# The low part of every weight split: 11/16 of the columns on VectorE, 5/16 on GpSimd

## The chip, the cores and the metric

The kernel runs on one core of one Trainium2 chip. The metric is the device time of a run in microseconds (us), taken as the median of three runs.

## What is computed

Two transformer blocks of two layers each, one after the other, on 256 tokens of 2048 features, everything in float32. Cut to what matters here:

```python
# first block, per layer
mod = silu(c) @ w_mod + b_mod                    # shift, scale, gate: c is one vector
h = rms_norm(x, g_pre) * (1 + scale) + shift
proj = h @ w_in                                  # 2048 x 5648
y = concat(sliding_window_attention, spatial_gating, gated_linear_attention) * silu(z)
x = x + gate * rms_norm(y @ w_out, g_post)
# second block, per layer
proj = rms_norm(x) @ w_in_2
x = x + concat(mla, differential, banded attention) @ w_o_2
h = rms_norm(x)
x = x + square(relu(h @ w_up_2)) @ w_down_2      # 2048 x 8192 and back
```

The weights are read once; with 256 tokens each weight is used for two token tiles of 128.

## The kernel before

**The products.** A float32 product is made of three faster ones. Each operand is split into a high part (hi, the value rounded to the type `fp32r`) and a low part (lo, the value less hi), and `three` (L285) adds hi x hi, hi x lo and lo x hi into one bank of PSUM (lines L287, L288, L289; L288 is the one that reads the weight's lo). In the MLP's `up` the weight is the stationary operand, and lines L1190 (hi) and L1192 (lo) do the same in two matmuls. Five of the 16 K tiles of the first layer are not split and go whole through L325.

**The weight units.** `w_unit` (L269) fetches two K tiles (128 rows each) times n columns (512, 288 or 264) into one raw tile [128, 1024] and calls `split` (L262), which makes hi on ScalarE (L265) and lo on VectorE (L266):

```python
        A.copy(out=hi[:, :n], in_=src)
        V.tensor_tensor(out=lo[:, :n], in0=src, in1=hi[:, :n].bitcast(F32), op=SUB)
```

There are 964 such splits. raw has 5 buffers, hi and lo have 3 each, so ScalarE and VectorE can be at most three units ahead of TensorE, and a raw buffer is free for the next load once its hi and lo are made. SP issues all of these loads from one queue, in order.

**The background work.** Beside the products of the first block, `gemv` (L475) computes the modulation vectors of the next stage on VectorE: it loads w_mod into rawm (2 buffers, the same SP queue, L485) and multiplies and adds into gacc (L491, L493), with both inputs in SBUF. `pump` gives out such a load after every four K tiles.

**Who else uses GpSimd.** `rstd` (L237) takes its power there (L241, 128x1 or 128x4), and four affine selects (L846) mask the spatial gate's weights; a few small loads are issued from its queue.

**What sets the order.** The program is written layer by layer, but the order in which each engine gets its instructions is made by a scheduler from its own estimates, so that a changed instruction can move its neighbours. All engines then run in their own order and wait for each other through semaphores.

Of the kernel before, what the change touches and what calls it, by code (L numbers as in the profile page):

```python
# [11 lines left out]
F32 = mybir.dt.float32  # L12
# [6 lines left out]
PSUM = bass.MemoryType.PSUM  # L19
# [71 lines left out]
def kernel(  # L91
# [36 lines left out]
    def gate_load(t, on):  # L128
        """a load into t waits for what on waits for."""
        V.tensor_copy(out=t[0:1, 0:1], in_=on)  # L130
# [4 lines left out]

    # ---------------------------------------------------------------- constants
    C_RES = C_SWA
# [17 lines left out]

    # vectors that scale features, feature-major
    fm = const.tile([P, 3 * P], F32, name="fm")
    fmap = {}

    def fm_load(g, parts, on=None):  # L160
        """parts: (names, [rows, 128] AP); the rows become columns of fm, from 128 g on."""
        st = tm("y")
        if on is not None:
            gate_load(st, on)
        n = 0
        for names, ap in parts:
            r = ap.shape[0]
            (nc.sync if g == 0 else nc.scalar).dma_start(out=st[n:n + r, :P], in_=ap)
            for i, name in enumerate(names):
                fmap[name] = g * P + n + i * (r // len(names))  # L170
            n += r
        pb = bank()
        PE.transpose(pb[:, :n], st[:n, :P], ident[:n, :n])
        V.tensor_copy(out=fm[:, g * P:g * P + n], in_=pb[:, :n])
# [17 lines left out]

    # vectors along the free axis
    sink_bc = const.tile([P, DEPTH, 16], F32, name="sink_bc")
# [34 lines left out]

    # ---------------------------------------------------------------- helpers  # L230
    def copy(eng, out, in_):
# [12 lines left out]
    def put(dst, ps, scale=None):  # L244
        """dst (hi | lo) from a [128, 256] view of PSUM."""
        hi, lo = dst[:, 0, :], dst[:, 1, :]
        if scale is None:
            A.copy(out=hi, in_=ps)
            V.tensor_tensor(out=lo, in0=ps, in1=hi.bitcast(F32), op=SUB)
        else:  # L250
            A.activation(out=hi, in_=ps, func=AF.Copy, scale=scale)
            V.scalar_tensor_tensor(out=lo, in0=ps, scalar=scale, in1=hi.bitcast(F32), op0=MUL, op1=SUB)  # L252
# [6 lines left out]
    def raw_tile(tag="raw"):  # L259
        return wp.tile([P, 1024], F32, tag=tag, bufs={"raw": 5, "rawm": 2}[tag], name=f"{tag}{next(uid)}")  # L260

    def split(src, n):  # L262
        hi = wp.tile([P, 1024], F32R, tag="hi", name=f"hi{next(uid)}")
        lo = wp.tile([P, 1024], F32R, tag="lo", name=f"lo{next(uid)}")
        A.copy(out=hi[:, :n], in_=src)  # L265
        V.tensor_tensor(out=lo[:, :n], in0=src, in1=hi[:, :n].bitcast(F32), op=SUB)  # L266
        return hi, lo

    def w_unit(w, k0, n0, n, whole=()):  # L269
        """4 K tiles x n columns of w, split but for those in whole; yields (kt, [(hi [128, n], lo), ...])."""  # L270
        for k in range(k0, k0 + 4, 2):
            raw = raw_tile()
            nc.sync.dma_start(
                out=raw[:, :2 * n].rearrange("p (k n) -> p k n", k=2),
                in_=w[k * P:(k + 2) * P, n0:n0 + n].rearrange("(k p) n -> p k n", p=P))
            js = [j for j in range(2) if k + j not in whole]
            parts = [(raw[:, j * n:(j + 1) * n], None) for j in range(2)]
            if js:
                o = js[0] * n
                hi, lo = split(raw[:, o:o + len(js) * n], len(js) * n)  # L280
                for i, j in enumerate(js):
                    parts[j] = hi[:, i * n:(i + 1) * n], lo[:, i * n:(i + 1) * n]
            yield (k, parts)

    def three(ps, xa, xb, wh, wl, first, last):  # L285
        """(xa + xb)^T (wh + wl) onto ps."""
        PE.matmul(ps, lhsT=xa, rhs=wh, start=first, stop=False)  # L287
        PE.matmul(ps, lhsT=xa, rhs=wl, start=False, stop=False)  # L288
        PE.matmul(ps, lhsT=xb, rhs=wh, start=False, stop=last)  # L289
# [4 lines left out]
    def settle(age=0):  # L294
        """the last step of each gemv whose loads were all given out at least age pumps ago."""
        while late and bg["n"] - late[0][0] >= age:
            late.pop(0)[1]()
# [42 lines left out]
    def softmax(ps, nh, nk, bias, scale, sink=None, rd=None):  # L340
        """ps [128, nh, nk]; bias: list of (head slice, AP); e = exp(s - max), 1 / sum.

        A sink is one more score, which no value goes with."""
        w = nk if sink is None else nk + 1
# [16 lines left out]
    def turn(srcs, eng, m=None, tag="k"):  # L361
        """transposes of up to 4 [128, 128] APs, side by side."""
        pb = bank()
        for j, a in enumerate(srcs):
            if m is None:
                PE.transpose(pb[:, j * P:(j + 1) * P], a, ident)  # L366
            else:
                PE.matmul(pb[:, j * P:(j + 1) * P], lhsT=a, rhs=m, start=True, stop=True)
        o = tm(tag)
        copy(eng, o[:, :len(srcs) * P], pb[:, :len(srcs) * P])  # L370
        return o

    def y_turn(dst, ytm):
        """ytm: per token tile a [128, 512]; dst: 4 act tiles."""
        for jj in range(0, 4, 2):
# [9 lines left out]
    def x_done(t, n):  # L385
        """the sum of squares of a finished 512-column piece of x."""
        if n == 0:
            ssx[t] = small(4)
        j = junk
        A.activation(out=j, in_=X[t][n], func=AF.Square, accum_out=ssx[t][:, n:n + 1])  # L390
# [5 lines left out]

    # rotary tables of the first block
    rope = const.tile([P, 2, 2, 16], F32, name="rope")
# [60 lines left out]
    def rotate(buf, nh, cos2, sin2, hf):  # L459
        """in place on buf [128, nh, 2 * hf]; sin2 = (-sin | sin)."""  # L460
        m1 = half_tile() if nh * 2 * hf <= S else tm("s")
# [9 lines left out]

    # ---------------------------------------------------------------- modulation
    mod = {}

    def gemv(l, part, k0, nk, eng, tag, into=None):  # L475
        """columns of (shift, scale, gate)[part] for K tiles k0 .. k0 + nk, feature-major; yields per load."""
        if (l, part) not in mod:
            mod[l, part] = const.tile([P, KT], F32, name=f"mod{l}_{part}")
        n = nk * P
        per = 1024 // n  # L480
# [32 lines left out]
    def gemv_pe(l, part, k0, nk, tag, pb):  # L513
        """the same on the tensor engine, a K tile of the result after the other, into a bank."""
        for i in range(nk):
# [10 lines left out]

    # ---------------------------------------------------------------- first block
    def swa_keys(kv):
# [8 lines left out]
    def swa(l, cc, q, kv, kT, zs, yT):  # L537
        """heads 8 cc .. 8 cc + 7."""
        ys = []
# [34 lines left out]
    def gla(l, qk, vg, cg, zs, yT):  # L574
# [35 lines left out]
        def decay(lv):  # L610
            """exp of level lv's exponents, [128 (head pair's keys), (tile, pair), token]."""
            eb = bank()
# [81 lines left out]
    def head_norm(hs, gain, z=None):  # L694
        """rms over each of 4 [128, 128] APs, times gain (times z)."""
        j = junk
# [44 lines left out]
    def make_hT(l, n, rb, hT, whole):  # L741
        """K tiles 4 n .. 4 n + 3 of the modulated, normalised x, feature-major."""
        for jj in range(0, 4, 2):
# [18 lines left out]
    def block1(l, phases, split_k, order, prepare, need_gate, whole=()):  # L762
# [19 lines left out]
        def places(name, t, ps):  # L782
            """where the columns of a chunk go: (name, tile, source)."""
            if name == "v0":
# [130 lines left out]

    # ---------------------------------------------------------------- second block
    def x_turn(n, gname, dst):
        """K tiles 4 n .. 4 n + 3 of x times a gain, feature-major."""
        for jj in range(0, 4, 2):
# [10 lines left out]
    def attend(nheads, score, bias, scale, vals, dst, m=None):  # L930
        """softmax attention over chunk-causal keys; outputs feature-major, 128 values per head."""
        for h0 in range(0, nheads, 4):
# [27 lines left out]
    def block2(l, xT, r):  # L960
        # c_q, c_kv, k_rope
        units = (0, 4, 8, 12)
# [118 lines left out]

        # differential heads
        for j in range(1, 3):
# [46 lines left out]

        # banded heads, queries of a tile in reverse order
        pr = [[None] * 3 for _ in range(2)]
# [38 lines left out]

        # MLP
        r2 = []
# [58 lines left out]
    def small2(t):  # L1232
        """(cos | cos | -sin | sin) of the second block's rotary positions."""
        o = rope2_t[t]
        return o
# [13 lines left out]

    # ---------------------------------------------------------------- the stack  # L1250
    spill = dr.tile([S, D], F32, name="spill")
# [119 lines left out]
```

## Time and profile before

| what | us |
|---|---|
| median of 3 runs | 3048.32 |
| lowest and highest run | 3045.58, 3050.96 |
| profiled execution, span from its first to its last instruction | 3045.1 |

For the profiled execution the profile gives the span alone; it lies 3.2 us under the median. All times of the trace are microseconds from the start of that span. The first block takes 0 to about 915 us, the first layer of the second block 915 to about 1980 us (its MLP from about 1225 on) and the last layer the rest (its MLP from about 2285 on). In the rows, PE is TensorE's matmuls and PEld its weight loads, DVE is VectorE, ACT ScalarE, POOL GpSimd, SP the engine whose queue issues the loads. A matmul's shown length includes its way through the array, so consecutive ones overlap; their pace is the distance of their starts.

### The profile page before, as it was taken

The numbers are of one execution on the slowest core, as the hardware profiler recorded it, in microseconds if no ns is written. First come the engines' busy times: TensorE is split into PE (matmuls) and PEld (weight loads), VectorE is DVE, ScalarE is ACT, GpSimd is POOL, SyncE is SP. The second block draws the span as 40 slices with busy tenths as digits, with TensorE's granted clock in tenths as the row PEclk, the third lists the DMA queues.
The fourth block names the chain that finished last, engine by engine and source line by source line (L and its number), as shares of the span: only waits on it lengthen the run. The fifth ranks groups of instructions, "written<-read, shape, count | busy, mean of one in ns | idle before, by whom it ended". The sixth has DMA issues, their size and how long they took to land.

```text
span 3045.1 us, 40015 instructions
## 1 busy us (share of the span) xinstructions
PE 2953.5 (97%) x15042; PEld 2442.3 (80%) x15042; DVE 1984.3 (65%) x2832; ACT 1436.1 (47%) x2271; POOL 36.3 (1%) x56
## 2 busy tenths in 40 slices
PE   6999998999999999999999999999999999999998
PEld 5676676887787887888888888888788888888887
DVE  5888877788766555565666656656555665656655
ACT  2334545445556555454444444455554444444444
POOL 0000000000000000000000000000000000000000
PEclk9999998999999999999999999999999999999999
DMA  8898588898454655565665566554556666555564
GB/s 286 291 317 291 184 266 288 279 309 269 123 180 146 180 145 163 175 188 192 189 191 188 190 190 190 190 173 135 166 165 199 192 188 190 190 190 190 188 191 153
DMA packets 318072, 617.57 MB, mean 203 GB/s; under 512 B 20233, under 2 KB 48069, under 8 KB 317877
## 3 DMA queue, kind: packets, MB, share of 16 engines
q1 hardware_dynamic: 317220, 614.40, 63.4%
q8 instruction: 118, 1.93, 0.3%
q0 software_dynamic: 336, 0.49, 0.1%
q14 instruction: 78, 0.63, 0.1%
q10 hardware_dynamic: 320, 0.12, 0.0%
HBM read 610.73 MB, written 4.19 MB: 202 GB/s over the span
## 4 chain that ended last, share of the span: by engine, by line
PE 80%; DMA 8%; DVE 7%; issue 2%; ACT 2%; POOL 0%; SPq 0%; DVEq 0%; ACTq 0%; POOLq 0%
PE b L288 16%; PE b L289 16%; PE b L287 16%; PE b L1190 16%; PE b L1192 8%; DMA rawm<-in_w_mod_dram 5%; DVE gacc L493 2%; DVE lo L266 2%; PE b L325 1%; DMA raw<-in_w_in_dram 1%; PE b L366 1%; ACT hi L265 1%; PE b L564 1%; PE b L952 1%; PE b L551 0%
## 5 line engine op out<-in xcount | busy, mean ns | idle before, releaser
L266 DVE TENSOR_TENSOR lo<-raw,hi 128x1024 fp32r<-128x1024 f32 (+4 forms) x964 | 1126.6, 1170 | 799.0 <-ACT hi L265 795.7
L265 ACT CAST hi<-raw 128x1024 fp32r<-128x1024 f32 (+4 forms) x964 | 972.7, 1009 | 1313.5 <-PE b L289 758.1
L287 PE MATMUL b<-hi,act 128*128 128x512 f32 (+2 forms) x2728 | 1072.9, 394 | 9.2 <-DVE pr L821 2.6
L288 PE MATMUL b<-lo,act 128*128 128x512 f32 (+2 forms) x2728 | 1047.7, 384 | 6.9 <-DVE lo L266 6.8
L289 PE MATMUL b<-hi,act 128*128 128x512 f32 (+2 forms) x2728 | 1045.5, 384 | 0.3 <-DVE act L252 0.3
L1190 PE MATMUL b<-act,hi 128*128 128x512 f32 x2048 | 721.0, 397 | 0.0
L287 PEld LDWEIGHTS b<-hi,act 128*128 128x128 f32 x2728 | 515.1, 189 | 121.2 <-issue 16.4
L288 PEld LDWEIGHTS b<-lo,act 128*128 128x128 f32 x2728 | 515.7, 189 | 117.1 <-DVE lo L266 11.7
L289 PEld LDWEIGHTS b<-hi,act 128*128 128x128 f32 x2728 | 514.9, 189 | 98.1 <-issue 1.2
L1192 PE MATMUL b<-act,lo 128*128 128x256 f32 x2048 | 574.9, 281 | 0.0
L1190 PEld LDWEIGHTS b<-act,hi 128*128 128x128 f32 x2048 | 384.4, 188 | 92.8
L1192 PEld LDWEIGHTS b<-act,lo 128*128 128x128 f32 x2048 | 386.9, 189 | 0.5
L493 DVE SCALAR_TENSOR_TENSOR gacc<-rawm,sc,gacc 128x1024 f32<-128x1024 f32 (+1 forms) x210 | 220.9, 1052 | 57.7 <-DMA rawm<-in_w_mod_dram 56.2
L325 PE MATMUL b<-raw,act 128*128 128x512 f32 (+1 forms) x240 | 111.0, 561 | 0.0
L1208 DVE SCALAR_TENSOR_TENSOR act<-b,s,act 128x512 f32<-128x512 f32 x128 | 90.0, 744 | 5.7 <-PE b L289 5.7
L354 ACT ACTIVATE s<-s,s 128x128 f32<-128x128 f32 (+3 forms) x144 | 64.1, 447 | 40.3 <-DVE s L351 39.3
L241 POOL TENSOR_TENSOR s<-s,cs 128x1 f32<-128x1 f32 (+1 forms) x38 | 27.6, 730 | 2909.0 <-DVE s L239 2709.3
L325 PEld LDWEIGHTS b<-raw,act 128*128 128x128 f32 x240 | 43.8, 191 | 17.9 <-issue 11.8
L1200 DVE SCALAR_TENSOR_TENSOR h<-h 128x256 f32<-128x256 f32 x128 | 54.4, 425 | 4.4
L821 DVE TENSOR_TENSOR act<-b,act 128x512 f32<-128x512 f32 (+2 forms) x82 | 51.4, 632 | 8.2 <-PE b L325 7.4
L390 ACT ACTIVATE junk<-act 128x512 bf16<-128x512 f32 x56 | 35.1, 626 | 40.2 <-DMA act<-in_x_dram 21.1
L1198 DVE TENSOR_TENSOR h<-b,h 128x256 f32<-128x256 f32 x128 | 53.4, 417 | 0.0
(268 smaller groups left out, 1666.7 us busy)
## 6 DMA issues: line engine op xcount, KB each, us to landing
raw<-in_w_in_dram SPq DMA_DIRECT2D x256, 512.0 KB, 4.8
raw<-in_w_up_dram SPq DMA_DIRECT2D x256, 512.0 KB, 3.7
raw<-in_w_down_dram SPq DMA_DIRECT2D x256, 512.0 KB, 3.6
rawm<-in_w_mod_dram SPq DMA_DIRECT2D x176, 512.0 KB, 4.8
raw<-in_w_out_dram SPq DMA_DIRECT2D x64, 512.0 KB, 4.7
raw<-in_w_o_dram SPq DMA_DIRECT2D x64, 512.0 KB, 3.7
raw<-in_w_in_dram SPq DMA_DIRECT2D x32, 288.0 KB, 2.9
raw<-in_w_in_dram SPq DMA_DIRECT2D x32, 264.0 KB, 4.7
```

Of the source, the lines that this page charges most:

```text
L265: A.copy(out=hi[:, :n], in_=src)
L266: V.tensor_tensor(out=lo[:, :n], in0=src, in1=hi[:, :n].bitcast(F32), op=SUB)
L287: PE.matmul(ps, lhsT=xa, rhs=wh, start=first, stop=False)
L288: PE.matmul(ps, lhsT=xa, rhs=wl, start=False, stop=False)
L289: PE.matmul(ps, lhsT=xb, rhs=wh, start=False, stop=last)
L325: PE.matmul(ps[t][:, :n], lhsT=a[:, t * P:(t + 1) * P], rhs=wh, start=kk + j == units[0], stop=kk + j == units[-1] + 3)
L354: A.activation(out=s[:, h, :], in_=s[:, h, :], func=AF.Exp, bias=nm[:, h:h + 1], accum_out=den[:, h:h + 1])
L493: eng.scalar_tensor_tensor(out=acc, in0=w, scalar=sc[:, u + k:u + k + 1], in1=acc, op0=MUL, op1=ADD)
L1190: PE.matmul(ps[f], lhsT=wh[:, f * P:(f + 1) * P], rhs=a.rearrange("p a b -> p (a b)"), start=(kk + j == 0), stop=False)
L1192: PE.matmul(ps[f][:, S:], lhsT=wl[:, f * P:(f + 1) * P], rhs=a[:, 0, :], start=False, stop=(kk + j == KT - 1))
L1200: V.scalar_tensor_tensor(out=s2, in0=s, scalar=0.0, in1=s, op0=MAX, op1=MUL)
L1208: V.scalar_tensor_tensor(out=xc, in0=ps, scalar=r2[t], in1=xc, op0=MUL, op1=ADD)
```

## The change

`split` is the only place that changes in what is executed. m is 704 of 1024 columns, 352 of 512, 363 of 528 and 182 of 264; VectorE subtracts those and GpSimd the last 320, 160, 165 or 82. Below this place the lines of the changed kernel are 5 higher, the hi copy is L267, VectorE's subtract L269 and GpSimd's L271. The rest of the diff removes comments and docstrings.

```diff
+    POOL_PART = 5
+
     def split(src, n):
         hi = wp.tile([P, 1024], F32R, tag="hi", name=f"hi{next(uid)}")
         lo = wp.tile([P, 1024], F32R, tag="lo", name=f"lo{next(uid)}")
         A.copy(out=hi[:, :n], in_=src)
-        V.tensor_tensor(out=lo[:, :n], in0=src, in1=hi[:, :n].bitcast(F32), op=SUB)
+        m = n - n * POOL_PART // 16
+        V.tensor_tensor(out=lo[:, :m], in0=src[:, :m], in1=hi[:, :m].bitcast(F32), op=SUB)
+        if m < n:
+            G.tensor_tensor(out=lo[:, m:n], in0=src[:, m:], in1=hi[:, m:n].bitcast(F32), op=SUB)
         return hi, lo
```

The order of instructions changes too. GpSimd's queue, late in the first layer, before (powers for a norm, two selects, two powers):

```order
14 L241 TENSOR_TENSOR s_2675<-s_2673,cs 128x4
15 L241 TENSOR_TENSOR s_2690<-s_2688,cs 128x4
16 L846 AFFINE_SELECT s_3234<-s_3234 128x512
17 L846 AFFINE_SELECT s_3245<-s_3245 128x512
18 L241 TENSOR_TENSOR s_3272<-s_3270,cs 128x1
19 L241 TENSOR_TENSOR s_3296<-s_3294,cs 128x1
```

And the same place of the changed kernel:

```order
94 L241 TENSOR_TENSOR s_2763<-s_2761,cs 128x4
95 L271 TENSOR_TENSOR lo_3201<-raw_3198,hi_3200 128x320
96 L271 TENSOR_TENSOR lo_3220<-raw_3217,hi_3219 128x160
97 L271 TENSOR_TENSOR lo_3246<-raw_3243,hi_3245 128x320
98 L271 TENSOR_TENSOR lo_3265<-raw_3262,hi_3264 128x160
99 L271 TENSOR_TENSOR lo_3286<-raw_3283,hi_3285 128x320
100 L851 AFFINE_SELECT s_3318<-s_3318 128x512
101 L851 AFFINE_SELECT s_3329<-s_3329 128x512
102 L271 TENSOR_TENSOR lo_3423<-raw_3420,hi_3422 128x320
103 L241 TENSOR_TENSOR s_3356<-s_3354,cs 128x1
104 L271 TENSOR_TENSOR lo_3442<-raw_3439,hi_3441 128x320
105 L241 TENSOR_TENSOR s_3380<-s_3378,cs 128x1
```

The subtracts of all 964 splits now stand between the powers and the selects, in one queue with them.

TensorE, one unit in the second layer of the first block, before, with the semaphores that a matmul waits for:

```order
1679 L287 MATMUL b_4284<-hi_4288,act_4231 128x512 [waits Activation_49]
1680 L288 MATMUL b_4284<-lo_4289,act_4231 128x512
1681 L289 MATMUL b_4284<-hi_4288,act_4231 128x512 [waits DVE_49]
1682 L287 MATMUL b_4284<-hi_4288,act_4236 128x512 [waits Activation_49]
1683 L288 MATMUL b_4284<-lo_4289,act_4236 128x512
```

And a unit at about the same place in the changed kernel (L292 to L294 are the three matmuls):

```order
1716 L292 MATMUL b_4400<-hi_4465,act_4392 128x512 [waits Activation_49]
1717 L293 MATMUL b_4400<-lo_4466,act_4392 128x512 [waits DVE_49]
1718 L294 MATMUL b_4400<-hi_4465,act_4392 128x512 [waits DVE_49]
1719 L292 MATMUL b_4400<-hi_4465,act_4397 128x512 [waits Activation_49]
1720 L293 MATMUL b_4400<-lo_4466,act_4397 128x512 [waits Pool_49]
```

The wait for GpSimd stands at the second matmul that reads lo, three matmuls after the first.

SP's queue of loads in the first layer, before:

```order
66 L273 DMA raw_884<-in_w_in_dram 128x2x512
67 L273 DMA raw_912<-in_w_in_dram 128x2x512
68 L485 DMA rawm_856<-in_w_mod_dram 128x2x512
69 L485 DMA rawm_898<-in_w_mod_dram 128x2x512
70 L273 DMA raw_930<-in_w_in_dram 128x2x512
71 L273 DMA raw_956<-in_w_in_dram 128x2x512
72 L485 DMA rawm_902<-in_w_mod_dram 128x2x512
```

And now:

```order
66 L278 DMA raw_905<-in_w_in_dram 128x2x512
67 L490 DMA rawm_876<-in_w_mod_dram 128x2x512
68 L278 DMA raw_934<-in_w_in_dram 128x2x512
69 L490 DMA rawm_920<-in_w_mod_dram 128x2x512
70 L278 DMA raw_953<-in_w_in_dram 128x2x512
71 L490 DMA rawm_924<-in_w_mod_dram 128x2x512
72 L278 DMA raw_980<-in_w_in_dram 128x2x512
```

Pairs of raw loads and pairs of rawm loads have become single ones in turn, so every second raw load stands one place later.

## Rows read from the trace of the kernel before

**Rows 1.** The page, part 1: busy us (share of the span) xinstructions.

```profile
PE 2953.5 (97%) x15042; PEld 2442.3 (80%) x15042; DVE 1984.3 (65%) x2832; ACT 1436.1 (47%) x2271; POOL 36.3 (1%) x56
```

**Rows 2.** Windows by stage: length, busy us by engine, granted clock, DMA share, GB/s.

```profile
76.00:915.00 839.00, 802.58 (x4030) 623.22 (x4030) 668.05 (x1047) 398.66 (x692) 16.43 (x21) 0.98 0.77 254
915.00:1225.00 310.00, 296.76 (x1614) 251.28 (x1613) 184.24 (x306) 174.37 (x345) 6.95 (x10) 0.98 0.53 157
1225.00:1980.00 755.00, 755.00 (x3808) 639.60 (x3807) 453.49 (x555) 338.42 (x440) 1.11 (x2) 1.00 0.60 189
```

**Rows 3.** Chain of waits, 76 to 915 us: share of the stretch by line.

```profile
by line: DMA rawm<-in_w_mod_dram 19.5%; PE b L288 8.8%; PE b L289 8.5%; PE b L287 8.5%; DVE gacc L493 7.6%; issue 6.3%; DVE lo L266 5.1%; DMA raw<-in_w_in_dram 4.8%; PE b L325 4.1%; PE b L564 2.0%; ACT hi L265 1.8%; PE b L551 1.7%; PE b L36
```

**Rows 4.** Waits of the SP queue, 76 to 915 us: us, times, longest.

```profile
SPq L273 <- DVE lo L266: 227.1, 121, 5.5
SPq L485 <- DVE gacc L493: 191.3, 107, 8.0
```

**Rows 5.** Waits for lo of TensorE's loads and matmuls, 76 to 915 us.

```profile
PEld b L288 <- DVE lo L266: 11.5, 15, 2.4
...
PE b L288 <- DVE lo L266: 6.8, 8, 1.9
```

**Rows 6.** Groups by form, VectorE, 76 to 915 us: busy us, mean ns, idle before.

```profile
L266 DVE TENSOR_TENSOR lo<-raw,hi 128x1024 fp32r<-128x1024 f32 x168 | 204.3, 1219 | 46.2 <-ACT hi L265 45.4
L493 DVE SCALAR_TENSOR_TENSOR gacc<-rawm,sc,gacc 128x1024 f32<-128x1024 f32 x120 | 153.6, 1280 | 45.8 <-DMA rawm<-in_w_mod_dram 45.4
L493 DVE SCALAR_TENSOR_TENSOR gacc<-rawm,sc,gacc 128x512 f32<-128x512 f32 x75 | 56.0, 747 | 9.7 <-DMA rawm<-in_w_mod_dram 9.0
...
L266 DVE TENSOR_TENSOR lo<-raw,hi 128x512 fp32r<-128x512 f32 x26 | 17.8, 684 | 3.5 <-ACT hi L265 3.3
...
L266 DVE TENSOR_TENSOR lo<-raw,hi 128x528 fp32r<-128x528 f32 x23 | 15.9, 700 | 2.1 <-ACT hi L265 2.1
...
L266 DVE TENSOR_TENSOR lo<-raw,hi 128x264 fp32r<-128x264 f32 x5 | 2.1, 428 | 0.8 <-ACT hi L265 0.8
```

**Rows 7.** Timeline, 390 to 396 us: start, us, engine line op; selects and a gacc.

```profile
392.84 0.64 POOL L846 TENSOR_SCALAR_AFFINE_SELECT s<-s 128x512 f32<-128x512 f32 x1 [28.82 <-DMA s<-in_sg_w_dram]
...
394.03 1.28 DVE L493 SCALAR_TENSOR_TENSOR gacc<-rawm,sc,gacc 128x1024 f32<-128x1024 f32 x1 [1.61 <-DMA rawm<-in_w_mod_dram]
...
394.90 0.91 POOL L846 TENSOR_SCALAR_AFFINE_SELECT s<-s 128x512 f32<-128x512 f32 x1 [1.42 <-DMA s<-in_sg_w_dram]
```

**Rows 8.** Timelines of GpSimd and VectorE: powers under a gacc and without.

```profile
518.33 0.55 POOL L241 TENSOR_TENSOR s<-s,cs 128x1 f32<-128x1 f32 x1 [113.08 <-DVE s L907]
1128.49 1.02 POOL L241 TENSOR_TENSOR s<-s,cs 128x4 f32<-128x4 f32 x1 [121.02 <-DVE s L239]
799.62 1.28 DVE L493 SCALAR_TENSOR_TENSOR gacc<-rawm,sc,gacc 128x1024 f32<-128x1024 f32 x1
799.85 1.92 POOL L241 TENSOR_TENSOR s<-s,cs 128x4 f32<-128x4 f32 x1 [271.93 <-DVE s L239]
```

**Rows 9.** The same about 519.6 us: a power under a two-input L911.

```profile
519.64 0.74 DVE L911 SCALAR_TENSOR_TENSOR act<-act,s,act 128x512 f32<-128x512 f32 x1
519.80 0.99 POOL L241 TENSOR_TENSOR s<-s,cs 128x1 f32<-128x1 f32 x1 [0.93 <-DVE s L239]
```

**Rows 10.** Timeline of TensorE in an MLP: first and last of 13 starts in turn.

```profile
1504.07 0.39 PE L289 MATMUL b<-hi,act 128*128 128x512 f32 x1
...
1506.79 0.39 PE L289 MATMUL b<-hi,act 128*128 128x512 f32 x1
```

**Rows 11.** Timelines of ScalarE and VectorE in the same MLP.

```profile
1501.77 1.05 ACT L265 CAST hi<-raw 128x1024 fp32r<-128x1024 f32 x1 [1.67 <-PE b L289]
1500.14 1.23 DVE L266 TENSOR_TENSOR lo<-raw,hi 128x1024 fp32r<-128x1024 f32 x1 [1.49 <-ACT hi L265]
```

**Rows 12.** Waits, 915 to 1225 us: us, times, longest.

```profile
DVE lo L266 <- ACT hi L265: 76.6, 64, 6.0
```

## The prediction

> **What bounds the kernel now.** I read the page's busy shares first. TensorE is busy 97% of the span, VectorE 65%, ScalarE 47%, GpSimd 1% [rows 1]. Work taken off VectorE can therefore pay only where VectorE, and not TensorE, sets the pace, and the windows by stage say where that is [rows 2]. In the first MLP (1225 to 1980 us) TensorE has not one idle microsecond: 755.00 busy of 755.00. In the attention part ahead of it (915 to 1225) it idles 13.2 us. The last layer repeats both from 1980 us on. In the first block's two layers, 76 to 915 us, it idles 36.4 of 839 us, VectorE is busy 668 us (80%) and the DMA engines 77%. I call this stretch stage A; it is the only one with something to win or lose.
>
> The chain of waits inside stage A [rows 3] agrees: a loop of gate-vector loads (rawm, 19.5%) and the multiply-adds that free them (gacc, 7.6%) carries more of it than any matmul line; the low parts (lo) carry 5.1%. The SP queue's own waits show the loop from the other side [rows 4]: it stood 227.1 us until a lo had freed a raw buffer and 191.3 us until a gacc had freed a rawm buffer. TensorE itself hardly waits for a lo: 6.8 us in 8 waits, and 11.5 us in 15 of its weight loads [rows 5].
>
> **What VectorE gives up.** The order of GpSimd's instructions shows all 964 subtracts there, so the change does what its words say. Stage A has 222 of them [rows 6]: 168 of 1024 columns (1219 ns), 26 of 512 (684 ns), 23 of 528, 5 of 264. Their slope is (1219 - 684)/512 = 1.045 ns a column, so 320 columns fewer save 0.334 us, 160 save 0.167, 165 save 0.172, 82 save 0.086. In stage A: 56.2 + 4.3 + 4.0 + 0.4 = 64.9 us, and VectorE falls from 668 to 603 us.
>
> **What GpSimd takes.** No subtract runs on it now. The nearest rows are the affine selects, one input, 512 columns, 0.64 us [rows 7], and the tiny powers of 0.55 us (1 column) and 1.02 us (4 columns) [rows 8]. The disturbed select started at 394.90 and took 0.91 us, to 395.81, under a gacc that ended at 394.03 + 1.28 = 395.31: 0.50 us of column work after it, and so a lead of 0.14 us and 0.98 ns a column. Lower bound for 320 columns: that rate, 0.14 + 0.31 = 0.45 us. Upper bound: double the rate for the second input and a whole power of 0.55 us as the lead, 1.18 us. I take double the rate with the lead of 0.14, 0.77 us, because lead and rate come from one instruction with tiles of this size; 0.63 us of it reads data. In stage A that is 168 x 0.63 + 26 x 0.31 + 23 x 0.32 + 5 x 0.16 = 122 us of reading. The Trainium skill (GPSIMD Engine Reference, "Elementwise — side-by-side cycle accounting") gives 4497 ns for a two-input add of 2048 columns; by it an estimate for 320 columns is 0.70 us, and the sum would hardly move. No run here shows that figure yet.
>
> **Do the two engines run side by side?** The trace says no, at least in one direction. A four-column power started 0.23 us into a gacc (two inputs in SBUF) and took 1.92 us for 1.02; it ended 0.87 us after that gacc did (799.85 + 1.92 = 801.77, against 799.62 + 1.28 = 800.90), and 0.87 is 1.02 less the lead of 0.14 to a hundredth [rows 8]. A one-column power under a two-input L911 took 0.99 for 0.55 us and ended 0.41 us after it, 0.55 less 0.14 [rows 9]. With the select that makes three: GpSimd stands still until VectorE's two-input instruction is through. The reverse, VectorE standing while GpSimd reads, has no row. The Trainium skill (SBUF — State Buffer, "Who interferes with whom") has it: whichever starts first holds a shared read port for its whole instruction and the other fully blocks. By that rule my sum below stands at +9.2 us; by the rows alone, which bind GpSimd only, it would be the faster rival's -15 us.
>
> Either way the two pieces run one after the other, since GpSimd waits for VectorE's: 1219 - 334 = 885 ns, then 0.63 us, together 1.51, and the whole lo of 1024 columns is 0.29 us later than now, not earlier. I take the reverse to hold too, since a port that makes one side wait has no shown reason to spare the other; its price is the 0.63 us of a reading at most, its lower end nothing.
>
> **Where this costs nothing.** In the MLP units TensorE needs 12 matmuls x 0.227 us = 2.72 us [rows 10]. A buffer freed by it is refilled by ScalarE (1.05 us) and VectorE (1.23 us) [rows 11], and three sets of hi and lo leave two units, 5.44 us, for that: 3.1 us to spare. 0.29 us, or 0.84 at the upper bound, goes into it; cost 0. If that cover were gone, each unit would show its lateness. GpSimd's columns belong to the second K tile of a unit, and the order shows TensorE's new wait three matmuls after its first use of lo: 3 x 0.227 = 0.68 us more time where a unit has 1024 columns. The attention parts I also put at 0: VectorE stood 76.6 us in 64 waits for hi before a lo in the first of them [rows 12], over 1 us each time, which covers 0.29. The reordered loads of stage A move the same bytes, a raw load one place back and a rawm load one forward; 0, give or take 5 us.
>
> **Stage A, the sum.** VectorE gains 64.9 us of time and loses what it is blocked. L266 and L493 have two SBUF inputs and are 240 + 210 of 668 us [rows 6]. With VectorE 80% busy the next instruction is there and is of this kind in 0.8 x 0.67 = 0.53 of cases: 0.53 x 122 = 65 us. Its load stays as it is, and only the places on the chain count.
> - gacc: 7.6% of 839 us is 64 us, 50 instructions of 1.28. There are 222 subtracts for 195 large gaccs, so about one each; I let every second one meet half a reading (0.31 us): 50 x 0.5 x 0.31 = +7.8 us.
> - lo: 5.1% is 43 us, 35 instructions. Raw loads carry 4.8%, 40 us, by my estimate some 7 of about 6 us; there GpSimd's piece, 0.29 us later, frees the buffer: +2.0 us.
> - The other 28 lead into VectorE's next instruction: between -0.33 us (not blocked) and +0.29 (blocked), so -9 to +8 us; I take the middle, -0.6.
>
> Sum: +9.2 us on the profiled span of 3045.1, or 3054.3. That span is 3.2 us under the median of 3048.32 (the runs go from 3045.58 to 3050.96), so the forecast in the metric is 3057.5 us.
>
> **The rivals.**
> - *No difference (3048, from 3043 to 3054).* For it: TensorE is busy 96% of stage A, the 0.68 us of grace covers the 0.29, and VectorE's blocked time equals what it saved. Against it: SP waits on exactly these releases. A change of 0.2%, 6 us, is about what runs of this kernel can tell from none, and this case lies inside it.
> - *Faster (3034).* VectorE is never held up by GpSimd, only the reverse, which is all that the rows show. Then the 35 lo on the chain shorten by 0.33 us, -12 us, and some of the 18.3 us that TensorE's matmuls and weight loads wait for lo go, I say -3. It decides so if no two-input VectorE instruction lengthens and GpSimd's piece ends within 0.68 us of VectorE's. Against it: the symmetry that I take above.
> - *Much slower (3090).* GpSimd's request is passed over while VectorE runs gacc after gacc: two of them are 2.56 us, and lo is 0.29 + 2.56 - 0.68 = 2.2 us late. If that befalls 50 of 222 splits and half of each shows, it costs 55 us; with GpSimd at its upper bound (1.18 us, 246 us of it for stage A if all is serial) 603 + 246 = 849 us exceed the stage's 839. With either mixed in I put this case at +32 to +55.
>
> **How the numbers follow.** Forecast 0.38, no difference 0.36, faster 0.15, much slower 0.11. The first and last give slower by over 0.2%: 0.49; the same 0.36; faster 0.15. The range goes from 3040, which leaves out most of the faster case, to 3086, which leaves out half of the slowest.
>
> **What would show it.** GpSimd's L271 at about 0.77 us where VectorE is not reading two inputs, and lasting until 0.63 us after VectorE's piece where both start together; VectorE's L269 of 704 columns at 885 ns; some gaccs at 1.5 to 1.9 us instead of 1.28; stage A about 850 us, the MLPs still with TensorE at 100%. A subtract above 1.4 us, an idle TensorE in an MLP, or a stage A shorter than 830 us would prove me wrong.

## The result, and the profile after

The change makes the kernel slower: 3094.71 us (median of 4 runs, 3078.95 to 3097.73) against 3049.64 us of the kernel before on the same chip (4 runs, 3045.58 to 3051.85). The ratio is 1.0144, with a 95% interval from 1.0115 to 1.0173. The forecast of 3057.5 us had the sign right and a fifth of the size, and 3094.71 lies outside its range, which ended at 3086. The profiled execution of the changed kernel has a span of 3096.0 us, 50.9 more than before.

The page, part 1 (compare [rows 1]), and one group of its part 5, columns as in [rows 6]:

```profile
PE 2971.4 (96%) x15042; PEld 2452.7 (79%) x15042; DVE 1852.4 (60%) x2832; ACT 1440.0 (47%) x2271; POOL 1404.6 (45%) x1020
...
L257 DVE TENSOR_TENSOR act<-h,act 128x256 fp32r<-128x256 f32 x128 | 101.0, 809 | 0.0
```

The subtracts moved: VectorE is busy 132 us less, GpSimd 1368 us more. The last line is the first sign of a price. L257, which the change does not touch, took 418 ns before:

```profile
L257 DVE TENSOR_TENSOR act<-h,act 128x256 fp32r<-128x256 f32 x128 | 50.9, 418 | 0.0
```

To compare stages, I moved the limits of the windows by the delay of the same unit: the 240th hi cast starts 29.2 us later than before, the 360th 41.3 and the 720th 50.8. The changed kernel by stage, columns as in [rows 2]:

```profile
76.00:944.00 868.00, 816.17 (x4040) 630.28 (x4039) 670.09 (x1050) 400.03 (x695) 277.68 (x244) 0.96 0.75 247
944.00:1266.00 322.00, 300.59 (x1617) 254.33 (x1616) 170.47 (x307) 174.56 (x346) 134.21 (x104) 0.97 0.51 151
1266.00:2021.00 755.00, 755.00 (x3807) 639.03 (x3806) 401.34 (x554) 340.50 (x440) 422.78 (x273) 1.00 0.60 189
2021.00:2336.00 315.00, 303.12 (x1631) 255.96 (x1630) 162.48 (x281) 167.68 (x322) 139.45 (x107) 0.99 0.52 155
```

And the kernel before, in the last of these stages ([rows 2] have the other three):

```profile
1980.00:2285.00 305.00, 299.68 (x1628) 252.90 (x1627) 179.90 (x280) 167.97 (x322) 5.38 (x8) 1.00 0.54 161
```

Stage A grew from 839 to 868 us, the first attention part from 310 to 322, the second from 305 to 315; the MLP has its 755 us again, with TensorE busy in all of them. 29 + 12 + 10 = 51 us, the whole difference. In these three stages TensorE's idle time grew by 15.4, 8.2 and 6.6 us, together 30.2, and the same matmuls took 13.6, 3.8 and 3.4 us longer, together 20.8, at a lower granted clock (0.96 for 0.98 in stage A).

Stage A of the changed kernel, VectorE and GpSimd by form (compare [rows 6]):

```profile
L269 DVE TENSOR_TENSOR lo<-raw,hi 128x704 fp32r<-128x704 f32 x168 | 178.4, 1068 | 46.6 <-ACT hi L267 46.2
L498 DVE SCALAR_TENSOR_TENSOR gacc<-rawm,sc,gacc 128x1024 f32<-128x1024 f32 x120 | 162.3, 1353 | 64.6 <-DMA rawm<-in_w_mod_dram 64.4
L498 DVE SCALAR_TENSOR_TENSOR gacc<-rawm,sc,gacc 128x512 f32<-128x512 f32 x76 | 63.2, 831 | 9.3 <-DMA rawm<-in_w_mod_dram 8.7
...
L271 POOL TENSOR_TENSOR lo<-raw,hi 128x320 fp32r<-128x320 f32 x168 | 216.2, 1289 | 378.4 <-ACT hi L267 357.1 <-DVE act L826 6.3 <-DMA raw<-in_w_in_dram 5.6
```

704 columns take 1068 ns where 885 were forecast, and the gaccs are 73 and 84 ns longer than in [rows 6]. Who waits for lo in stage A (us, times, longest; compare [rows 5]):

```profile
PE b L293 <- DVE lo L269: 12.2, 13, 3.6
...
PE b L293 <- POOL lo L271: 0.2, 1, 0.2
...
PEld b L293 <- DVE lo L269: 18.1, 18, 3.8
```

TensorE's matmuls and weight loads wait 30.3 us for VectorE's lo (18.3 before) and its matmuls 0.2 us for GpSimd's. The late piece is VectorE's. The timeline of the changed kernel shows how, at two places (start, us, engine and line, idle time before it):

```profile
618.64 2.00 DVE L498 SCALAR_TENSOR_TENSOR gacc<-rawm,sc,gacc 128x1024 f32<-128x1024 f32 x1 [2.27 <-DMA rawm<-in_w_mod_dram]
618.68 0.88 POOL L271 TENSOR_TENSOR lo<-raw,hi 128x320 fp32r<-128x320 f32 x1 [1.58 <-ACT hi L267]
...
1605.80 0.89 DVE L269 TENSOR_TENSOR lo<-raw,hi 128x704 fp32r<-128x704 f32 x1
1605.80 1.61 POOL L271 TENSOR_TENSOR lo<-raw,hi 128x320 fp32r<-128x320 f32 x1 [1.33 <-ACT hi L267]
...
1606.61 1.10 DVE L257 TENSOR_TENSOR act<-h,act 128x256 fp32r<-128x256 f32 x1
```

At 618.68 GpSimd needs only its own 0.88 us, and the gacc that started just before it takes 2.00 us for 1.28, 0.72 more. At 1605.80 the two pieces of a split start together. GpSimd ends 0.72 us after VectorE's piece (1607.41 against 1606.69), so it waited and then read; the L257 behind that piece ends 0.30 us after GpSimd (1607.71), having taken 1.10 us for 0.42: it waited for the reading. Each engine stands still for the other.

Which of the two is held up goes by the start, but not to the last hundredth. In stage A a large gacc and a piece of 320 columns started within 0.15 us of each other eight times. The gacc was held up (by 0.61 to 0.72 us) in the four in which GpSimd started before it or at most 0.04 us after it, as at 618.64, and GpSimd (by 0.99 to 1.09 us) in the four in which it started 0.06 us or more after it, as here:

```profile
489.45 1.29 DVE L498 SCALAR_TENSOR_TENSOR gacc<-rawm,sc,gacc 128x1024 f32<-128x1024 f32 x1 [2.02 <-DMA rawm<-in_w_mod_dram]
489.51 1.96 POOL L271 TENSOR_TENSOR lo<-raw,hi 128x320 fp32r<-128x320 f32 x1 [1.35 <-ACT hi L267]
```

### The profile page after: what moved, and what is told of

Its sections match the earlier page's. It is cut to its first block, busy times and chain, and to the rows that moved or that the text cites. A ratio compares the mean times of both kernels' runs of the same rounds, so it can differ in the third digit from the quotient of the medians.

```text
span 3096.0 us, 42667 instructions
## 1 busy us (share of the span) xinstructions
PE 2971.4 (96%) x15042; PEld 2452.7 (79%) x15042; DVE 1852.4 (60%) x2832; ACT 1440.0 (47%) x2271; POOL 1404.6 (45%) x1020
## 5 line engine op out<-in xcount | busy, mean ns | idle before, releaser
L271 POOL TENSOR_TENSOR lo<-raw,hi 128x320 fp32r<-128x320 f32 (+4 forms) x964 | 1367.2, 1419 | 1540.5 <-ACT hi L267 1445.7
L267 ACT CAST hi<-raw 128x1024 fp32r<-128x1024 f32 (+4 forms) x964 | 970.9, 1008 | 1255.5 <-POOL lo L271 622.6
L269 DVE TENSOR_TENSOR lo<-raw,hi 128x704 fp32r<-128x704 f32 (+4 forms) x964 | 882.2, 918 | 923.9 <-ACT hi L267 918.8
L292 PE MATMUL b<-hi,act 128*128 128x512 f32 (+2 forms) x2728 | 1078.5, 396 | 7.8 <-ACT hi L267 2.9
L294 PE MATMUL b<-hi,act 128*128 128x512 f32 (+2 forms) x2728 | 1048.7, 385 | 3.1 <-DVE act L249 2.3
L292 PEld LDWEIGHTS b<-hi,act 128*128 128x128 f32 x2728 | 518.3, 190 | 120.1 <-issue 14.8
L294 PEld LDWEIGHTS b<-hi,act 128*128 128x128 f32 x2728 | 517.5, 190 | 102.9 <-DVE act L249 2.7
L498 DVE SCALAR_TENSOR_TENSOR gacc<-rawm,sc,gacc 128x1024 f32<-128x1024 f32 (+1 forms) x210 | 237.2, 1129 | 76.1 <-DMA rawm<-in_w_mod_dram 75.1
L257 DVE TENSOR_TENSOR act<-h,act 128x256 fp32r<-128x256 f32 x128 | 101.0, 809 | 0.0
L359 ACT ACTIVATE s<-s,s 128x128 f32<-128x128 f32 (+3 forms) x144 | 64.1, 447 | 47.5 <-DVE s L356 47.2
L1205 DVE SCALAR_TENSOR_TENSOR h<-h 128x256 f32<-128x256 f32 x128 | 61.7, 482 | 4.4
```

Source lines behind the costliest of these rows:

```text
L257: V.tensor_tensor(out=lo, in0=full, in1=hi.bitcast(F32), op=SUB)
L269: V.tensor_tensor(out=lo[:, :m], in0=src[:, :m], in1=hi[:, :m].bitcast(F32), op=SUB)
L271: G.tensor_tensor(out=lo[:, m:n], in0=src[:, m:], in1=hi[:, m:n].bitcast(F32), op=SUB)
L498: eng.scalar_tensor_tensor(out=acc, in0=w, scalar=sc[:, u + k:u + k + 1], in1=acc, op0=MUL, op1=ADD)
```

## The experiments

Four theories were set against each other: GpSimd's readings block VectorE (the expectations call this the port); lo is complete later (lateness); the scheduler's order is worse (order); GpSimd's queue holds up its other work (queue). Every edit is made to the changed kernel. The line that sets up the scratch tile `scr` (128x320) is left out below.

**A reading alone, in the order of before.** VectorE subtracts all columns; GpSimd reads as many as in the change into a scratch tile that nobody waits for.

```diff
-        V.tensor_tensor(out=lo[:, :m], in0=src[:, :m], in1=hi[:, :m].bitcast(F32), op=SUB)
+        V.tensor_tensor(out=lo[:, :n], in0=src, in1=hi[:, :n].bitcast(F32), op=SUB)
-            G.tensor_tensor(out=lo[:, m:n], in0=src[:, m:], in1=hi[:, m:n].bitcast(F32), op=SUB)
+            G.tensor_tensor(out=scr[:, :n - m], in0=cs[:, :n - m], in1=hi[:, m:n].bitcast(F32), op=SUB)
```

> VectorE subtracts all columns as in the kernel before, and GpSimd reads as many columns as in the change (hi and a constant) into a scratch tile that nobody reads; the engines' orders, apart from GpSimd's, are those of the kernel before. Port theory (GpSimd's reading and VectorE's two-input instructions shut each other out): slower than before by 30 to 80 us, at least as much as the change in the first block, since VectorE gets nothing back; gacc and lo show lengthened instructions. Order theory (the scheduler's other order, and splits that stand in GpSimd's queue behind its powers, cost the 45 us): within 6 us of before, because nobody waits for these subtracts and the order is the old one.

Measured: 3089.17 us, ratio 1.0118 [1.0104, 1.0133]. Its stage A and its form groups there:

```profile
76.00:944.00 868.00, 816.13 (x4030) 628.53 (x4029) 726.06 (x1048) 399.46 (x692) 292.27 (x242) 0.97 0.76 246
```

```profile
L270 DVE TENSOR_TENSOR lo<-raw,hi 128x1024 fp32r<-128x1024 f32 x167 | 230.4, 1384 | 34.3 <-ACT hi L268 34.0
L499 DVE SCALAR_TENSOR_TENSOR gacc<-rawm,sc,gacc 128x1024 f32<-128x1024 f32 x120 | 163.9, 1366 | 39.2 <-DMA rawm<-in_w_mod_dram 38.9
```

TensorE idles 51.9 us here and 51.8 in the changed kernel. No lo is late on GpSimd's account and no engine but GpSimd has another order, yet 1.18 of 1.44% are lost: the reading does it. The reading also keeps a hi buffer in use for longer, but nobody waits for that here: the copy that fills the same buffer again, three splits later, started 2.2 us or more after the end of the reading in all of stage A.

**The piece without a reading, in the changed kernel's order.** GpSimd writes zeros to its columns.

```diff
-            G.tensor_tensor(out=lo[:, m:n], in0=src[:, m:], in1=hi[:, m:n].bitcast(F32), op=SUB)
+            G.memset(lo[:, m:n].bitcast(F32), 0.0)
```

> GpSimd writes its columns of lo as zeros instead of subtracting, so it reads nothing; the part left out is the low half of 5/16 of each weight's columns. The orders of TensorE, VectorE, ScalarE and SP are those of the change to within 8 rows, and TensorE still waits for GpSimd's piece. Port theory: the loss is gone, within 6 us of before, or up to 20 us faster, since VectorE is 65 us lighter in the first block. Order theory: still 3085 to 3100 us.

Measured: 3047.55 us, ratio 0.9982 [0.9967, 0.9996]. Stage A, at the limits of before, and its forms:

```profile
76.00:915.00 839.00, 797.39 (x4055) 624.33 (x4054) 613.53 (x1051) 402.28 (x696) 91.39 (x245) 0.98 0.78 256
```

```profile
L498 DVE SCALAR_TENSOR_TENSOR gacc<-rawm,sc,gacc 128x1024 f32<-128x1024 f32 x120 | 153.8, 1282 | 64.1 <-DMA rawm<-in_w_mod_dram 63.6
L269 DVE TENSOR_TENSOR lo<-raw,hi 128x704 fp32r<-128x704 f32 x170 | 150.3, 888 | 69.3 <-ACT hi L267 56.4 <-POOL lo L271 6.3 <-issue 4.1
```

The new order costs nothing that shows, and GpSimd's writes lengthen neither gacc nor lo. VectorE is busy 54.5 us less in stage A than before (613.53 against 668.05), and this relief buys 4.1 us there (the 240th hi cast) and none at the end of the profiled span. The 0.18% by which the ratio lies under 1 is what another kernel of the same series showed, whose gain did not come again (the MLPs alone, below).

**As busy, hardly a reading.** GpSimd subtracts one column and writes the rest of its piece twice. This was meant to make lo as late as in the change, without a reading.

```diff
-            G.tensor_tensor(out=lo[:, m:n], in0=src[:, m:], in1=hi[:, m:n].bitcast(F32), op=SUB)
+            G.tensor_tensor(out=lo[:, m:m + 1], in0=src[:, m:m + 1], in1=hi[:, m:m + 1].bitcast(F32), op=SUB)
+            for _ in range(2):
+                G.memset(lo[:, m + 1:n].bitcast(F32), 0.0)
```

> The change's order, and GpSimd's piece of lo as late as in the change, but hardly any reading: it subtracts one column (which waits for hi and for VectorE's piece) and then writes the piece twice with zeros, 2 x 0.37 us. Left out: the low half of nearly 5/16 of each weight's columns. Theory that VectorE's blocked time is the loss: as the run that only writes, within 6 us of before. Theory that TensorE and the loads wait for the later piece: 3085 to 3100 us.

Measured: 3055.52 us, ratio 1.0016 [0.9995, 1.0036]. Stage A at the limits of before, and one unit in its MLP:

```profile
76.00:915.00 839.00, 795.64 (x4005) 621.40 (x4004) 607.76 (x1044) 396.26 (x689) 273.47 (x680) 0.97 0.77 253
```

```profile
1543.68 1.05 ACT L267 CAST hi<-raw 128x1024 fp32r<-128x1024 f32 x1 [1.77 <-PE b L1197]
...
1543.78 0.79 POOL L273 MEMSET lo<- 128x319 f32 x2 [0.90 <-PE b L1199]
...
1544.76 0.89 DVE L269 TENSOR_TENSOR lo<-raw,hi 128x704 fp32r<-128x704 f32 x1 [1.93 <-ACT hi L267]
1544.81 0.89 POOL L271 TENSOR_TENSOR lo<-raw,hi 128x1 fp32r<-128x1 f32 x1 [0.24 <-ACT hi L267]
```

The edit did not do what it was meant to. The writes need only a free buffer, and the scheduler put them ahead of the one-column subtract in 954 of the 964 splits. Here the zeros are in place at 1544.57, before hi is at 1544.73, and lo is complete at 1545.70, 0.97 us after hi and 0.05 us after VectorE's piece. In the changed kernel's split at 1605.80 that is 1.68 us after hi. So this run says nothing about lateness. What it does show is that GpSimd's queue is not the cause: GpSimd is busy 273.47 us in stage A, for 277.68 in the changed kernel, with its powers and selects in the same queue, and at most 0.36% is lost.

**A reading, not late, in the changed kernel's order.** GpSimd zeroes its columns and then reads as many into the scratch tile.

```diff
-            G.tensor_tensor(out=lo[:, m:n], in0=src[:, m:], in1=hi[:, m:n].bitcast(F32), op=SUB)
+            G.memset(lo[:, m:n].bitcast(F32), 0.0)
+            G.tensor_tensor(out=scr[:, :n - m], in0=cs[:, :n - m], in1=hi[:, m:n].bitcast(F32), op=SUB)
```

> The change's order, VectorE relieved as in the change, GpSimd's piece written early with zeros, and then as long a reading as in the change into a scratch tile that nobody waits for. Left out: the low half of 5/16 of each weight's columns. Blocked-time theory: 3085 to 3100 us, as the change. Lateness theory: within 6 us of before. Both in parts: in between, and the share of each is read off together with the late piece without reading.

Measured: 3088.41 us, ratio 1.0129 [1.0103, 1.0154]. Stage A:

```profile
76.00:944.00 868.00, 814.40 (x4050) 628.95 (x4049) 666.13 (x1051) 400.81 (x695) 334.05 (x468) 0.97 0.75 247
```

No piece of lo is late through GpSimd, and 1.29 of 1.44% are lost. With the first experiment, where nobody waits for GpSimd's result either, this is what speaks against lateness: 0.15 and 0.26% are left for it, less than the uncertainty of the ratios. VectorE's load is 666 us here and 726 in the first experiment, 60 us apart, and the loss is the same within the intervals. Between these two, how full VectorE is makes no difference that shows; that its instructions are stopped does.

**How much is read.** The share of GpSimd is 1/16 and 8/16.

```diff
-    POOL_PART = 5
+    POOL_PART = 1
```

> GpSimd takes 1/16 (64 of 1024 columns) in place of 5/16. Port theory: the reading falls from 0.73 us to some 0.15 us plus its lead, so the loss falls to about a quarter, 5 to 15 us over before. Queue theory (splits stand behind powers in GpSimd's queue, whatever their size): 35 to 45 us over before, as the change. Lateness theory (TensorE waits because GpSimd's piece ends later than VectorE's): 0 to 5 us.

> GpSimd takes 8/16 of the columns of every split. Theory of blocked readings: a piece of 512 columns reads for about 0.14 us less than its time, 0.73 x 512 / 320 = 1.17 us, and VectorE's two pieces 704 to 512 columns save only 0.2 us more; the loss grows with the columns that GpSimd reads, from 1.44% to between 1.9 and 2.9% (3108 to 3140 us). In the MLPs the lo is complete 0.51 + 0.14 + 1.17 us after hi, under the 3 us to spare: TensorE still has no idle time there. Rival (the loss is a fixed price of one more instruction and one more wait per split, not of the columns): the ratio stays at 1.012 to 1.017. Rival (GpSimd is the bound in the first block): over 3%.

Measured: 3062.72 us, ratio 1.0032 [1.001, 1.0055], with 1/16, and 3128.3 us, ratio 1.0251 [1.0228, 1.0275], with 8/16. The loss for each sixteenth is 0.32% (its interval is wide, 0.10 to 0.55), 0.29% (the change) and 0.31%: it grows with the columns read, so it is no fixed price of one more instruction or wait. In the MLP with 8/16, TensorE still has no idle time:

```profile
1320.00:2030.00 710.00, 710.00 (x3599) 602.03 (x3598) 335.00 (x522) 314.62 (x400) 451.50 (x259) 1.00 0.61 189
```

**Where.** 5/16 in one part of the program only; `where` is set at the start of each part. Two kernels, and the MLPs alone in two measurements.

```diff
-        m = n - n * POOL_PART // 16
+        m = n - n * POOL_PART // 16 if where["now"] in ON else n
```

> Only the first block's splits are shared with GpSimd. By the stage marks of the change's trace (27 us behind at the end of the first block): 3073 to 3083 us. If the loss in the attention parts were only a consequence of the first block's lateness: 3095.

> Only the splits of the second block's projections around its attention are shared (w_in, w_uq, w_ukv, w_o). By the stage marks (12 and 10 us in the two layers): 3068 to 3078 us. If the loss there depends on the first block: within 6 us of before.

> Only the splits of the two MLPs are shared with GpSimd (5/16), the others are VectorE's alone. All theories that place the loss in the first block and in the attention parts: within 6 us of before. If the MLP's own spans cost anything hidden in the trace, up to 20 us over before.

> The same edit as the run with 5/16 in the MLPs alone, which came out at a ratio of 0.998 with its interval just under 1. Theory of blocked readings: TensorE is never idle in an MLP, so neither relief nor blocking of VectorE can show; the ratio is 1.000, between 0.998 and 1.002, and the small gain of the first measurement was scatter. Rival (taking load off VectorE in the MLPs is worth something): the ratio is 0.998 again with an interval below 1.

Measured: the first block alone 1.0072 [1.0044, 1.01]; the second block's attention parts alone 1.0066 [1.0044, 1.0089]; the MLPs alone 0.9982 [0.9968, 0.9996] and, with more runs, 1.0008 [0.9993, 1.0024]. 0.72 + 0.66% is close to the whole 1.44. The MLPs give no difference, and the small gain of the first measurement did not come again, so none of these versions is shown to be faster than the kernel before.

## Why the prediction was wrong

**Right: each engine blocks the other.** The prediction's step "I take the reverse to hold too" is borne out by the two timelines above and by the second experiment, where a GpSimd that only writes leaves a gacc at 1282 ns. The rule of the Trainium skill (SBUF — State Buffer, "Who interferes with whom") agrees in both directions, and also in what it says of writers: a two-input instruction of VectorE contends with a GpSimd instruction that reads, not with one that only writes. The prediction took over from it that whichever starts first blocks the other; by the eight meetings above that holds only to within some 0.05 us. The faster rival is out.

**Right: "Its load stays as it is".** 668.05 us before, 670.09 after. The two sides of it were near, too: 64.9 us of relief forecast and 54.5 measured without a reading, on VectorE as a whole; 65 us blocked forecast and 56.6 measured (670.09 - 613.53).

**Right: the MLPs at 0.** GpSimd's piece there ends 1.61 us after both start, and TensorE never idles, not even with 512 columns.

**A little low: GpSimd's piece.** 0.87 us undisturbed where 0.77 was taken, and 0.72 us of reading for 0.63. This would lift the term of +7.8 to 8.9 and changes nothing else much.

**Wrong: the sum for stage A, +9.2 us for a measured 29.** The step that failed is the one that let gained and blocked time cancel. It priced the lo terms at +1.4 us together: +2.0 for a freed buffer, and for "the other 28" the middle, -0.6, between "-0.33 us (not blocked) and +0.29 (blocked)". Gained and blocked time do not cancel. The second experiment and the changed kernel have the same order, but for some two dozen instructions that moved by up to three places, and differ in the reading. In the profiled executions, without it the 240th hi cast starts 4.1 us earlier than before, with it 29.2 us later. So 54.5 us of relief bought 4.1 us and 56.6 us of blocking cost 33.3. Even with all 28 at their blocked end the sum gives 7.8 + 2.0 + 8 = 17.8 us.

Of the 29 us, 13.6 are the clock (below), for which the sum had no term, and 15.4 are idle time of TensorE. Of these 15.4 only 5.4 are its matmuls' waits for VectorE's lo (12.2 us for 6.8). The rest is spread over other waits, for gacc and h for example, which stood at 0.9 and 0.2 us before:

```profile
PE b L503 <- DVE gacc L498: 3.5, 2, 2.0
PE b L606 <- DVE h L604: 3.4, 2, 3.1
```

How the terms of the sum share the loss in the changed kernel stays open, because its chain of waits cannot be followed back into stage A. In the first experiment, which has the same loss there, it can (columns as in [rows 3]):

```profile
by line: DMA rawm<-in_w_mod_dram 16.9%; DVE gacc L499 8.1%; PE b L294 7.9%; issue 7.9%; PE b L293 7.6%; PE b L295 7.6%; DVE lo L270 7.5%; DMA raw<-in_w_in_dram 5.5%; PE b L331 2.4%; ACT hi L268 1.9%; PE b L570 1.7%; DVE act L827 1.6%; DVE k
```

Against [rows 3], lo went from 42.8 us (5.1% of 839) to 65.1 (7.5% of 868), gacc from 63.8 to 70.3, raw loads from 40.3 to 47.7 and issue from 52.9 to 68.6, while the rawm loads fell from 163.6 to 146.7 and the three matmul lines from 216.5 to 200.5. The +6.5 of gacc is near the +7.8 forecast. The +22.3 of lo is not the price in the changed kernel: here VectorE subtracts all columns and has no relief. It shows only that blocking alone puts lo on the chain for much longer.

Why the relief is worth so little was not tried by itself; the second experiment shows only that it is: VectorE's 704 columns are done in 888 ns, and it idles 23.1 us more than before ahead of them (69.3 for 46.2) and 18.3 us more ahead of the large gaccs (64.1 for 45.8) [rows 6], so most of what was saved turns up as waiting for something else.

**Wrong: "The attention parts I also put at 0".** They cost 12 and 10 us of the 51. The cover that I named, VectorE's waits for hi before a lo [rows 12], is real but covers only the lo. (Nor is it "over 1 us each time": 1.2 us is the mean of the 64 waits, and six of them were under 0.29 us.) There the blocked instructions that count are others: VectorE's steps between one matmul and the next. VectorE by form in the first attention part and the start of its MLP (930 to 1322 us), changed kernel, and below it the same of the kernel before (901 to 1281 us):

```profile
L900 DVE TENSOR_TENSOR act<-act,act 128x512 f32<-128x512 f32 x8 | 7.0, 890 | 0.1
...
L946 DVE TENSOR_TENSOR s<-s,s 128x512 f32<-128x512 f32 x9 | 6.6, 732 | 0.3
...
L354 DVE SCALAR_TENSOR_TENSOR s<-b,act 128x512 f32<-128x512 f32 x7 | 4.6, 686 | 6.2 <-PE b L1154 3.3 <-PE b L1111 2.8
...
L1123 DVE SCALAR_TENSOR_TENSOR s<-s,s,s 128x256 f32<-128x256 f32 x4 | 2.4, 638 | 0.0
```

```profile
L941 DVE TENSOR_TENSOR s<-s,s 128x512 f32<-128x512 f32 x9 | 6.2, 692 | 0.3
...
L895 DVE TENSOR_TENSOR act<-act,act 128x512 f32<-128x512 f32 x8 | 5.3, 686 | 0.0
...
L349 DVE SCALAR_TENSOR_TENSOR s<-b,act 128x512 f32<-128x512 f32 x7 | 4.6, 688 | 4.3 <-PE b L1106 2.3 <-PE b L1149 1.9
...
L1118 DVE SCALAR_TENSOR_TENSOR s<-s,s,s 128x256 f32<-128x256 f32 x4 | 1.7, 476 | 0.0
```

TensorE's waits for two of these steps in the same stretches, after and then before:

```profile
PE b L371 <- DVE s L1123: 6.1, 4, 2.7
...
PE b L373 <- DVE s L946: 3.1, 2, 2.8
```

```profile
PE b L368 <- DVE s L941: 1.8, 2, 1.7
PE b L366 <- DVE s L1118: 1.6, 2, 1.3
```

The steps whose inputs are all in SBUF (L946, L900, L1123; L941, L895, L1118 before) are longer, and TensorE waits 9.2 us for two of them where it waited 3.4, which is 5.8 of the 8.2 us by which its idle time grew in this part. L354, with one input in PSUM (b), keeps its 0.69 us.

**Not in the sum: the clock.** 20.8 of the 51 us are matmuls at a lower granted clock. By the trace's record of the clock, its lower level held for 64.9 us of stage A (37.5 before) and for 17.1 (10.2) and 6.8 (0) of the two attention parts, 41 us more in all; at half the pace that is 20.5 us. The timeline of the changed kernel's TensorE, and a window of 4 us behind it (columns as in [rows 2]):

```profile
774.05 0.40 PE L292 MATMUL b<-hi,act 128*128 128x512 f32 x1
774.29 0.39 PE L293 MATMUL b<-lo,act 128*128 128x512 f32 x1
777.76 1.04 PE L606 MATMUL b<-gate_up,h 17*128 17x256 f32 x2 [3.09 <-DVE h L604]
...
779.76 0.63 PE L293 MATMUL b<-lo,act 128*128 128x512 f32 x1
780.18 0.63 PE L294 MATMUL b<-hi,act 128*128 128x512 f32 x1
```

```profile
780.00:784.00 4.00, 4.00 (x10) 3.06 (x10) 3.17 (x5) 3.94 (x5) 1.59 (x1) 0.50 0.85 253
```

After TensorE had waited 3.09 us for VectorE the granted clock is 0.50, its lower level of 1.2 GHz, and matmuls start 0.42 us apart instead of 0.24. More waiting for VectorE goes with more time at that level. The two are seen together; no experiment took one without the other.

**The rivals.** "No difference" fell with stage A. "Much slower" gave 3090 us, near the result, but for reasons that did not happen: of the 167 pieces of 320 columns that started up to 930 us, 10 took over 1.7 us, the longest 2.63, and GpSimd is busy 277.68 of 868 us in stage A. "A subtract above 1.4 us" was no good test: waiting behind VectorE's piece alone makes 1.58, and the prediction's own 1.51 us for a split already lies above it.

## What to carry to other kernels

Giving part of a two-input instruction to a second engine did not relieve the first here, because the second one's reading stopped it. What counted was not the load of either engine but which instructions were stopped: those with someone waiting for them cost more than the freed time elsewhere gave back. Price such a move by listing every instruction of the first engine with the sensitive form in each stage, not only the one that moves, and ask of each who waits behind it. Test it by adding the suspected traffic alone, with its result unused: that showed 1.18 of the 1.44% here without touching the split.

## What the runs showed of the hardware

GpSimd's two-input subtract took 0.57 us for 160 columns and 0.87 us for 320, undisturbed:

```profile
316.54 0.87 POOL L271 TENSOR_TENSOR lo<-raw,hi 128x320 fp32r<-128x320 f32 x1 [7.34 <-ACT hi L267]
...
349.48 0.57 POOL L271 TENSOR_TENSOR lo<-raw,hi 128x160 fp32r<-128x160 f32 x1 [19.47 <-ACT hi L267]
```

That is 1.9 ns a column and some 0.27 us besides; for all 320 columns the figure of the Trainium skill (GPSIMD Engine Reference, "Elementwise — side-by-side cycle accounting") had given an estimate of 0.70 us, 0.17 too little.

Not expected: a VectorE instruction with one tensor input from SBUF was lengthened as well. L1122, 256 columns with scalar operands, took 350 ns on average before (as L1117) and 520 after:

```profile
L1122 DVE TENSOR_SCALAR s<-s,s 128x256 f32<-128x256 f32 x4 | 1.9, 520 | 0.1
```

```profile
L1117 DVE TENSOR_SCALAR s<-s,s 128x256 f32<-128x256 f32 x4 | 1.2, 350 | 0.1
```

The mean hides two kinds. Of the eight in the changed kernel six took 0.35 us and two 1.03, and those two began within 0.03 us of a GpSimd piece that took its undisturbed 0.86 us. In the run that reads without being late, two of eight took 0.95 us, both begun 0.21 us after the start of a reading. Where GpSimd only writes, none is longer. No experiment took this instruction by itself.
